# A hybrid decoder step on one core: the renewal of the recurrent states begins four weight slabs later and is spread over more slabs

## The chip, the core and the metric

The kernel runs on one core of a Trainium2 chip. The core has a matrix engine (TensorE, PE in the profile, with its weight loads listed apart as PEld), three engines for elementwise work (VectorE, DVE; ScalarE, ACT; GpSimd, POOL) and SyncE (SP), which here only issues DMA transfers. Each engine works through its own list of instructions in order, and they wait for each other by semaphores. Tiles lie in the on-chip memory SBUF; matmul results go to PSUM. The metric is the device time of one execution in microseconds (us), as a median over runs.

## The reference

One decoder layer, for 256 prompt tokens and 8 sample sequences of 8 tokens each (320 tokens in all), with a model width of 2048. Cut to what matters:

```python
def decoder_layer(x, ssm_state, ssm_conv_state, ffn_conv_state, p):
    h = rms_norm(x, p["norm_mix_pre"])
    proj = h @ p["w_in"]
    a_u, a_v, z, xbc, dt_raw = ...                      # columns of proj
    gate_out, chunk_v = chunk_spatial_gate(a_u, a_v, ...)
    ssm_out, new_ssm, new_ssm_conv = ssd_mixer(z, xbc, dt_raw, ssm_state, ...)
    mix = jnp.concatenate([gate_out, ssm_out], axis=-1) @ p["w_out"]
    x = x + rms_norm(mix, p["norm_mix_post"])
    f, new_ffn_conv = conv_ffn(rms_norm(x, p["norm_ffn_pre"]), ffn_conv_state, ...)
    return x + rms_norm(f, p["norm_ffn_post"]), new_ssm, ...

def conv_ffn(h, conv_state, w_up, conv_w, conv_b, w_down):
    up = h @ w_up                                       # 2048 -> 2 * 5632
    up, new_conv = causal_depthwise_conv(up, conv_state, conv_w, conv_b)   # 3 taps
    g, u = jnp.split(up, 2, axis=-1)
    return (jax.nn.gelu(g, approximate=True) * u) @ w_down, new_conv
```

Inside `ssd_mixer` each sample sequence has a recurrent state of 32 heads x 64 x 128 numbers. By the recurrence `h_t = exp(dt_t a) h_{t-1} + dt_t x_t B_t^T` over its eight tokens, the new state is the old one times a factor per head and sequence, plus a product of the token rows x and B. This new state is only an output; nothing in the layer reads it. The change concerns the work that makes it, called the renewal below.

## The kernel before, in words

**Weights in slabs.** Nearly all of the time goes into four large products. Their weights are float32, and each block of 128x128 is multiplied in three matmuls: `whi` by the high part of the activations (L143), `whi` by their low part (L144) and `wlo` by their high part (L145). The weights come in slabs of 512 KB. `slab()` issues one load on SP (L126, tile `wraw`), has ScalarE cast it to `whi` (L130) and VectorE subtract that from `wraw` to give `wlo` (L132). There are three buffers of each of these tiles, so at most three slabs are under way. One slab feeds 24 matmuls of 320 columns.

**The ConvFFN stage.** It runs from about 800 us to the end and has eleven groups of 512 columns. `ffn_up(g)` makes a group's up-projection in two halves, eight slabs each. After a half four accumulators in PSUM (`ps`) are evacuated, each by `evac`: POOL prepares the edges of the tile `pad` (L1084, L1085), VectorE multiplies the accumulator into it (L1087, L1088), ScalarE makes the first tap of the convolution (L1094) and VectorE two more (L1096, into `gcv` or `ucv`), POOL copies the last columns out (L1098, L1099), and gelu, product and split into `fhi` and `flo` follow. There are four PSUM banks for this, so the next half's accumulators wait until VectorE has read the old ones. `chunk_out(g)` is the down-projection of a group, eight slabs, whose results VectorE adds to `acc_ffn` (L236). The order is up(0), up(1), out(0), up(2), out(1) and so on: 24 slabs to a round.

**Work in the background.** A generator in the list `bg` is advanced by one step (`tick`) behind every slab; so each `yield` in it means "go on behind the next slab". In this way small work is placed between the slabs of large work. Slab loads, casts and subtractions are emitted at high priority and so stand a few slabs ahead of their matmuls in each engine's list.

**The renewals.** `renewals()` is such a generator. It is put into `bg` behind `ffn_up(0)`. It first finishes three prompt states (L1163, six yields), then issues on SP the load of `tote`, the factors of all heads (L1183), of the first four states (L1171, tile `st`, 256 KB each) and of the token rows (L1180, tile `xb`). Then, for each of four groups: it waits three slabs, ScalarE copies the token rows into `xb_parts` (L1191), VectorE completes these in two operations (L1194); and for each of two halves, POOL multiplies four states by their factors (L1199, one slab apart), the next states' loads are issued on SP, two slabs pass, TensorE makes the four products `up_ps` (L1211), VectorE adds each to its state (L1213) and ScalarE's queue stores it (L1215). States have four buffers for the first halves and two sets of three, shared with older tiles, for the second ones, so a load waits until the store of an older state has landed. All multiplications need `tote`.

A call of `finish(grow)` ahead of the last group would work off what is left of the generator at once; it comes behind 240 ticks. Before the change the generator ends at the 103rd.

Of the kernel before, what the change touches and what calls it, by code (L numbers as in the profile page):

```python
# [34 lines left out]
def hybrid_step(  # L35
# [21 lines left out]
    def misc(name):  # L57
        return ms.tile([P, 512], F32, tag="ms", name=name)
# [328 lines left out]
    def by_head(ap):  # L387
        return ap.rearrange("p (h d) -> p h d", d=64)
# [674 lines left out]
    with tc.tile_pool(name="fp", bufs=1) as fp:  # L1063
# [91 lines left out]
        def renewals():  # L1155

            raw = hp.tile([P, 4, NT], F32R, tag="ohi", name="xb").bitcast(F32).rearrange("p k n -> p (k n)").rearrange("p (h c) -> p h c", h=2)
            part = hp.tile([P, 4, NT], F32R, tag="olo", name="xb_parts").rearrange("p k n -> p (k n)").rearrange("p (h c) -> p h c", h=2)
            tote = fp.tile([P, NH, NB], F32, name="tote")
            for g, s1, x1d, _ in rest:  # L1160
                yield from repeat(None, 2)
                with tc.issue_after(rsqrt_ins[-1]):
                    dve.tensor_tensor(out=s1, in0=s1, in1=x1d, op=ALU.add)  # L1163
                act.dma_start(o_ssm_p[g], s1)

            def load(g, h):

                st = [fp.tile([P, 512], F32, tag="st", name="st", bufs=4) if h == 0 else
                      cp.tile([P, 512], F32, tag=("s1", "x1d")[i % 2], name="st", bufs=3) for i in range(4)]
                for i in range(4):  # L1170
                    sp.dma_start(st[i], state_ssm[4 * h + i, g])  # L1171
                return st

            def tokens(g):

                rows = xb_d[g].rearrange("(h i t) c -> i t h c", h=2, i=4)
                for i in range(4):
                    for r in range(4):
                        at = 32 * i + TS * r
                        sp.dma_start(raw[at:at + TS], rows[i])  # L1180

            with tc.issue_after(slab_load[-1]):
                sp.dma_start(tote, tote_d)  # L1183
                ahead = [load(0, 0)]
            yield
            with tc.issue_after(slab_load[-1]):
                tokens(0)
            for g in range(4):
                h0 = 8 * g
                yield from repeat(None, 3)  # L1190
                act.copy(part, raw)  # L1191
                yield
                for at, m in ((slice(0, 512), 0), (slice(512, 640), 1)):
                    dve.scalar_tensor_tensor(out=part[:, :, at], in0=part[:, :, at].bitcast(F32), scalar=low[:, m:m + 1], in1=raw[:, :, at],  # L1194
                                             op0=ALU.mult, op1=ALU.add)
                for h in range(2):
                    st = ahead.pop(0)
                    for i in range(4):
                        pool.tensor_tensor(out=by_head(st[i]), in0=by_head(st[i]),  # L1199
                                           in1=tote[:, h0:h0 + 8, 4 * h + i:4 * h + i + 1].to_broadcast([P, 8, 64]), op=ALU.mult)  # L1200
                        yield
                    if h == 0:
                        ahead.append(load(g, 1))
                    elif g < 3:
                        ahead.append(load(g + 1, 0))
                        tokens(g + 1)
                    yield from repeat(None, 2)
                    grown = [misc("up_ps") for _ in range(4)]
                    for i in range(4):
                        at = slice(32 * i, 32 * i + 32)  # L1210
                        pe.matmul(grown[i], part[at, h, 512:], part[at, h, :512], start=True, stop=True, tile_position=(32 * i, 0))  # L1211
                    for i in range(4):
                        dve.tensor_tensor(out=st[i], in0=st[i], in1=grown[i], op=ALU.add)  # L1213
                        yield
                        act.dma_start(o_ssm_s[4 * h + i, g], st[i])  # L1215

        NG = NF // 4
        nxt = ffn_up(0)
        grow = renewals()
        bg.append(grow)  # L1220
        for g in range(NG):
# [173 lines left out]
```

## Time and profile before

| | us |
|---|---|
| median of 3 runs | 1760.93 |
| lowest and highest run | 1760.37 and 1761.53 |
| the profiled execution, its own time | 1762.04 |
| its span, first to last instruction | 1760.3 |
| granted TensorE clock, mean | 0.999 |

The profile lists busy time by engine over the span. In a row of the timeline stand the start and the length in us, the engine, the line in the code, the operation, what it writes and reads, the shape, and how many instructions of the kind run without another in between; in brackets the idle time of the engine ahead of it and what ended that. DVE's share over the whole run is 66%, ACT's 46% and POOL's 15%. The 32 multiplications of L1199 take 41.0 us in all, the 32 additions of L1213 20.6 us, the eight operations of L1194 7.7 us and the 32 products of L1211 4.0 us.

### The profile page before, as it was taken

To read this page: it belongs to the slowest core of one execution; us is meant where nothing else is said; L and a number is where in the kernel's file an instruction comes from. 1 tells how busy PE (TensorE), PEld (TensorE's weight loads), DVE (VectorE), ACT (ScalarE), POOL (GpSimd) and SP (SyncE) were. 2 spreads that over 40 slices of the span, in tenths; PEclk is the share of its full clock that TensorE was granted. 3 is DMA by queue.
4 is the path that set the end of the run, shared out by engine and by line. 5 is a ranking of instruction groups with operands and counts; after the bars stand their busy time and mean duration, and the time that the engine had idled before them with its cause. 6 is when DMAs were issued, how large, how long until landed. Compare 5 with 4: busy or idle time off the path is not lost.

```text
span 1760.3 us, 31124 instructions
## 1 busy us (share of the span) xinstructions
PE 1751.6 (100%) x12178; PEld 1729.8 (98%) x12178; DVE 1154.1 (66%) x1949; ACT 806.6 (46%) x1172; POOL 272.7 (15%) x588
## 2 busy tenths in 40 slices
PE   9999999999999999999999999999999999999998
PEld 9999999999999999999999999999999999999997
DVE  7449754656767576668966677676657565656575
ACT  7344545333854445545544434343434343333335
POOL 1003200000111101021331212130201010111004
PEclk9999999999999999999999999999999999999999
DMA  7466655456665644554756666756454545454542
GB/s 248 144 167 182 185 151 150 153 155 190 216 206 163 201 145 131 166 161 143 228 169 223 189 217 195 222 185 192 151 153 148 156 148 155 148 155 147 155 151 104
DMA packets 228179, 301.38 MB, mean 171 GB/s; under 512 B 19936, under 2 KB 150848, under 8 KB 227840
## 3 DMA queue, kind: packets, MB, share of 16 engines
q1 hardware_dynamic: 215856, 281.27, 52.4%
q10 hardware_dynamic: 10640, 13.60, 2.2%
q0 software_dynamic: 1536, 4.52, 1.0%
q8 instruction: 96, 1.57, 0.4%
q14 instruction: 51, 0.42, 0.1%
HBM read 283.47 MB, written 15.61 MB: 170 GB/s over the span
## 4 chain that ended last, share of the span: by engine, by line
PE 95%; DVE 2%; DMA 1%; ACT 0%; POOL 0%; issue 0%; SPq 0%; POOLq 0%; DVEq 0%; ACTq 0%
PE ps L143 20%; PE ps L145 20%; PE ps L144 20%; PE pd L143 10%; PE pd L144 10%; PE pd L145 10%; PE y_ps L900 1%; DMA wraw<-in_ffn_w_up 1%; DVE wlo L132 1%; PE yo_ps L848 0%; PE sg L705 0%; PE tsum L284 0%; DVE h_lo L374 0%; DVE acc_mix L1042 0%; DMA vt<-in_xT 0%; ACT whi L130 0%
## 5 line engine op out<-in xcount | busy, mean ns | idle before, releaser
L132 DVE TENSOR_TENSOR wlo<-wraw,whi 128x1024 fp32r<-128x1024 f32 x470 | 582.9, 1241 | 436.9 <-ACT whi L130 434.9
L130 ACT CAST whi<-wraw 128x1024 fp32r<-128x1024 f32 x470 | 492.0, 1047 | 730.3 <-PE ps L144 437.7
L143 PE MATMUL ps<-h_hi,whi 128*128 128x320 f32 x2528 | 782.1, 310 | 0.4 <-ACT whi L130 0.4
L144 PE MATMUL ps<-h_lo,whi 128*128 128x320 f32 x2528 | 779.8, 309 | 0.0
L145 PE MATMUL ps<-h_hi,wlo 128*128 128x320 f32 x2528 | 777.8, 309 | 0.0
L143 PEld LDWEIGHTS ps<-h_hi,whi 128*128 128x128 f32 x2528 | 474.8, 188 | 4.2 <-issue 2.3
L144 PEld LDWEIGHTS ps<-h_lo,whi 128*128 128x128 f32 x2528 | 475.1, 188 | 0.0
L145 PEld LDWEIGHTS ps<-h_hi,wlo 128*128 128x128 f32 x2528 | 474.4, 188 | 0.1
L143 PE MATMUL pd<-fhi,whi 128*128 128x320 f32 x704 | 217.2, 309 | 0.0
L144 PE MATMUL pd<-flo,whi 128*128 128x320 f32 x704 | 217.0, 308 | 0.0
L145 PE MATMUL pd<-fhi,wlo 128*128 128x320 f32 x704 | 216.9, 308 | 0.0
L143 PE MATMUL pd<-ohi,whi 128*128 128x320 f32 x448 | 139.5, 312 | 0.0
L145 PE MATMUL pd<-ohi,wlo 128*128 128x320 f32 x448 | 138.5, 309 | 0.0
L144 PE MATMUL pd<-olo,whi 128*128 128x320 f32 x448 | 138.5, 309 | 0.0
L143 PEld LDWEIGHTS pd<-fhi,whi 128*128 128x128 f32 x704 | 132.2, 188 | 0.7 <-issue 0.7
L144 PEld LDWEIGHTS pd<-flo,whi 128*128 128x128 f32 x704 | 132.2, 188 | 0.2 <-issue 0.2
L145 PEld LDWEIGHTS pd<-fhi,wlo 128*128 128x128 f32 x704 | 132.2, 188 | 0.0
L1099 POOL COPY ptf<-pad 128x2 f32<-128x2 f32 x88 | 24.2, 275 | 508.3 <-DVE pad L1087 507.5
L236 DVE TENSOR_TENSOR acc_ffn<-acc_ffn,pd 128x320 f32<-128x320 f32 x160 | 77.2, 482 | 34.5 <-PE pd L145 33.6
L143 PEld LDWEIGHTS pd<-ohi,whi 128*128 128x128 f32 x448 | 84.0, 188 | 1.4 <-issue 0.7
L144 PEld LDWEIGHTS pd<-olo,whi 128*128 128x128 f32 x448 | 84.1, 188 | 0.2 <-issue 0.2
L145 PEld LDWEIGHTS pd<-ohi,wlo 128*128 128x128 f32 x448 | 84.1, 188 | 0.0
(301 smaller groups left out, 1513.6 us busy)
## 6 DMA issues: line engine op xcount, KB each, us to landing
wraw<-in_ffn_w_up SPq DMA_DIRECT2D x176, 512.0 KB
wraw<-in_w_in SPq DMA_DIRECT2D x142, 512.0 KB
wraw<-in_ffn_w_down SPq DMA_DIRECT2D x88, 512.0 KB
wraw<-in_w_out SPq DMA_DIRECT2D x64, 512.0 KB
st<-in_state_ssm SPq DMA_DIRECT2D x64, 256.0 KB
out_ssm_state_sample<-st ACTq DMA_DIRECT2D x32, 256.0 KB
cs<-dacs_d SPq DMA_DIRECT2D x16, 320.0 KB
xr<-in_xT SPq DMA_DIRECT2D x4, 640.0 KB
```

The lines of the kernel that those rows point to most:

```text
L130: act.copy(hi[:, :m], raw[:, :m])
L132: dve.tensor_tensor(out=lo[:, :m], in0=raw[:, :m], in1=hi[:, :m].bitcast(F32), op=ALU.subtract)
L143: pe.matmul(ps, whi, xhi, start=first, stop=False)
L144: pe.matmul(ps, whi, xlo, start=False, stop=False)
L145: newest[0] = pe.matmul(ps, wlo, xhi, start=False, stop=last).ins
L236: dve.tensor_tensor(out=acc[:, nb, :], in0=acc[:, nb, :], in1=ps[:, :NT], op=ALU.add)
L900: pe.matmul(ps[64 * i:64 * i + 64, cols], w(hl), x(hl, m, cpx), tile_position=(0, 64 * i), **flags)
L1099: pool.tensor_copy(ptf[:, k, :], pad[:, 256:258])
```

## The change

Three edits in `renewals()`, all of them yields:

```diff
@@ renewals()
                 act.dma_start(o_ssm_p[g], s1)
+            yield from repeat(None, 4)
...
             for g in range(4):
                 h0 = 8 * g
-                yield from repeat(None, 3)
+                yield from repeat(None, 3 if g else 12)
                 act.copy(part, raw)
                 yield
...
                         pool.tensor_tensor(out=by_head(st[i]), in0=by_head(st[i]),
                                            in1=tote[:, h0:h0 + 8, 4 * h + i:4 * h + i + 1].to_broadcast([P, 8, 64]), op=ALU.mult)
                         yield
+                        yield
```

The loads of `tote`, the states and the token rows are placed four slabs later; the first copy of the token rows is placed twelve slabs behind them instead of three; and two slabs, not one, pass at each multiplication. The generator now ends at the 148th tick. No operation is added or taken away. A line is added ahead of the loads, so line numbers behind it rise by one in the changed kernel, and by two behind the third edit (the loads are L1184, L1172 and L1181, the multiplications L1200, the products L1213 there).

Each engine's list is the same in kind and number; the places change. On SP, this is where `tote`, the first states and the first token rows are issued, beside the weight loads `wraw`. Before:

```order
L126 DMA wraw<-in_ffn_w_up 128x2x512 x2
L126 DMA wraw<-in_ffn_w_up 128x4x256
L1183 DMA tote<-tote_d 128x256
L1171 DMA st<-in_state_ssm 128x512 x3
L126 DMA wraw<-in_ffn_w_up 128x4x256
L1171 DMA st<-in_state_ssm 128x512
L1180 DMA xb<-xb_d 8x2x640
```

After:

```order
L126 DMA wraw<-in_ffn_w_up 128x2x512 x2
L126 DMA wraw<-in_ffn_w_up 128x4x256
L1172 DMA st<-in_state_ssm 128x512
L126 DMA wraw<-in_ffn_w_up 128x4x256
L1172 DMA st<-in_state_ssm 128x512
L126 DMA wraw<-in_ffn_w_up 128x2x512 x3
L1184 DMA tote<-tote_d 128x256
L1172 DMA st<-in_state_ssm 128x512 x2
L126 DMA wraw<-in_ffn_w_up 128x2x512
L1172 DMA st<-in_state_ssm 128x512 x2
L1181 DMA xb<-xb_d 8x2x640
```

`tote` stands four weight loads later. Two states are now loaded ahead of it.

On POOL, these are the first multiplications, among the preparation of `pad` and the copies from it. Before:

```order
L1084 MEMSET pad 128x2
L1085 COPY pad<-fst 128x8x2
L1199 TENSOR_TENSOR st<-st,tote 128x512 x5
L1084 MEMSET pad 128x2
L1085 COPY pad<-fst 128x8x2
L1199 TENSOR_TENSOR st<-st,tote 128x512 x3
L1099 COPY ptf<-pad 128x2
L1098 COPY stg<-pad 128x16
```

After:

```order
L1084 MEMSET pad 128x2
L1085 COPY pad<-fst 128x8x2
L1200 TENSOR_TENSOR st<-st,tote 128x512
L1098 COPY stg<-pad 128x16
L1099 COPY ptf<-pad 128x2
L1200 TENSOR_TENSOR st<-st,tote 128x512 x4
L1098 COPY stg<-pad 128x16
L1099 COPY ptf<-pad 128x2
L1200 TENSOR_TENSOR st<-st,tote 128x512 x3
L1099 COPY ptf<-pad 128x2
L1098 COPY stg<-pad 128x16
L1200 TENSOR_TENSOR st<-st,tote 128x512
```

Eight multiplications stood together, ahead of the copies of a half's tiles; now ten (the last one stands behind one more preparation of `pad`) stand among the copies of the next half's tiles.

On VectorE, these are the two operations on `xb_parts`, among the subtractions that make `wlo`, behind the end of group 1's evacuation. Before:

```order
L371 TENSOR_TENSOR flo<-a,fhi 128x320
L132 TENSOR_TENSOR wlo<-wraw,whi 128x1024 x2
L1194 TENSOR_SCALAR xb_parts<-xb_parts,low,xb 128x2x512
L1194 TENSOR_SCALAR xb_parts<-xb_parts,low,xb 128x2x128
L132 TENSOR_TENSOR wlo<-wraw,whi 128x1024
L1213 TENSOR_TENSOR st<-st,up_ps 128x512 x4
```

After:

```order
L371 TENSOR_TENSOR flo<-a,fhi 128x320
L132 TENSOR_TENSOR wlo<-wraw,whi 128x1024 x6
L1195 TENSOR_SCALAR xb_parts<-xb_parts,low,xb 128x2x512
L1195 TENSOR_SCALAR xb_parts<-xb_parts,low,xb 128x2x128
L132 TENSOR_TENSOR wlo<-wraw,whi 128x1024 x6
```

They stand four slabs later, and the additions that need the first products no longer follow one slab behind them. On TensorE the first four products stood in the sixth slab of `chunk_out(0)`; they now stand three slabs into the second half of `ffn_up(2)`, fourteen slabs later. Without them TensorE's list is the same row for row.

## The prediction

> **What bounds the kernel now.** I read the page first, then the busy time by stretches, then TensorE's waits.
>
> ```profile
> PE 1751.6 (100%) x12178; PEld 1729.8 (98%) x12178; DVE 1154.1 (66%) x1949; ACT 806.6 (46%) x1172; POOL 272.7 (15%) x588
> ...
> 920.00:950.00 30.00, 29.41 (x202) 28.94 (x201) 23.72 (x38) 17.61 (x30) 6.32 (x15) 1.00 0.61 193
> ...
> 1150.00:1250.00 100.00, 100.00 (x683) 99.12 (x682) 66.08 (x108) 40.68 (x51) 15.44 (x49) 1.00 0.56 173
> 1250.00:1350.00 100.00, 100.00 (x684) 100.00 (x683) 59.42 (x98) 39.04 (x47) 12.86 (x40) 1.00 0.49 150
> ```
>
> Behind each stretch stand its length and the busy time of PE, PEld, DVE, ACT and POOL. TensorE is busy throughout at full clock. 684 matmuls in 100 us are one every 0.146 us; a slab (one 512 KB weight load) feeds 24 of them, so TensorE eats a slab in 3.51 us. The renewals run from 853 to 1229 us. The stretch with them (1150 to 1250) has 683 matmuls, the one after them 684, and in both TensorE is never idle. So whatever the change does, time can come only from an idle gap of TensorE that goes, or go into a new one. Its waits, whole run, longest first (total, times, longest):
>
> ```profile
> PE early L70 <- DVE ones L66: 1.1, 1, 1.1
> PE tsum L284 <- DVE sq L302: 0.7, 1, 0.7
> PE up_ps L1211 <- DVE xb_parts L1194: 0.6, 1, 0.6
> PE ps L143 <- ACT whi L130: 0.4, 1, 0.4
> ```
>
> Only one of them belongs to the renewals: 0.6 us, once. That is the most the change can win, 0.03% of the run.
>
> **Part 1: the wait that goes.** Here is that gap, in the timeline:
>
> ```profile
> 938.08 2.48 DVE L1194 SCALAR_TENSOR_TENSOR xb_parts<-xb_parts,low,xb 128x1024 fp32r<-128x1024 f32 x2 [0.26 <-DMA wraw<-in_ffn_w_up]
> 938.89 2.60 POOL L1199 TENSOR_TENSOR st<-st,tote 128x512 f32<-128x512 f32 x2 [8.41 <-DMA st<-in_state_ssm]
> ...
> 940.71 0.50 PE L1211 MATMUL up_ps<-xb_parts 32*128 32x512 f32 x4 [0.59 <-DVE xb_parts L1194]
> ```
>
> VectorE's two operations on xb_parts end at 940.56, and the first group of up_ps matmuls, already next on TensorE, waits 0.59 us for them. In the changed order these two operations stand behind four more slabs on VectorE, but the first up_ps group stands some fourteen slabs later on TensorE, so about ten slabs (35 us) more lie between them. The wait goes whole: minus 0.6. What is late next there is nothing: TensorE's weights are ready.
>
> **Part 2: what only moves.** The 32 up_ps matmuls, the xb casts on ScalarE, the 32 additions on VectorE and the 32 stores are the same in number; without up_ps, TensorE's order is the same row for row. I cost these at nothing. Their cover is the lead with which weights are made ready. It can be read from an undisturbed piece after the last renewal:
>
> ```profile
> 1229.15 0.37 SPq L126 DMA_DIRECT2D wraw<-in_ffn_w_up  x1
> ...
> 1237.20 1.03 ACT L130 CAST whi<-wraw 128x1024 fp32r<-128x1024 f32 x1
> ...
> 1247.46 1.05 ACT L130 CAST whi<-wraw 128x1024 fp32r<-128x1024 f32 x1 [2.47 <-PE ps L144]
> ...
> 1248.54 1.23 DVE L132 TENSOR_TENSOR wlo<-wraw,whi 128x1024 fp32r<-128x1024 f32 x1 [2.29 <-ACT whi L130]
> ```
>
> A cast starts when TensorE lets go of the slab three back (1247.46); two slabs, 7.0 us, then lie ahead of the new one, and its wlo is read two matmuls (0.3) in, at 1254.7. It is made at 1249.77: 4.9 us early. If VectorE or ScalarE lose less than 4.9 us together, TensorE sees nothing; each us beyond costs one.
>
> The state loads on SP wait until the store that frees their buffer has landed, and weight loads queue behind them. SP's waits in 850 to 1300 us say how long:
>
> ```profile
> SPq L1171 <- DMA out_ssm_state_sample<-st: 14.8, 8, 4.4
> ```
>
> At most 4.4 us at once, and TensorE felt none of it. A weight load is issued 8.05 us ahead of its cast (1229.15 to 1237.20, the same slab) and needs about 4.8 us to land (the figure of tote below, my estimate for a slab), so 3.2 us of lateness are free and 4.9 more before TensorE stops. In the new order the loads again stand two or three slabs behind their stores. Cost nothing; if a block grew beyond 8 us, it would cost the rest. The end of the chain moves from the 103rd slab behind ffn_up(0) to the 148th; the call that would finish it by force comes after the 240th, so nothing is left over for it.
>
> **Part 3: what the first multiplications meet.** This is the term that decides. All of POOL's multiplications wait for tote, then run in a bunch. Before:
>
> ```profile
> 870.97 0.37 SPq L126 DMA_DIRECT2D wraw<-in_ffn_w_up  x1
> 871.39 0.50 SPq L1183 DMA_DIRECT2D tote<-tote_d  x1
> ```
> ```profile
> 876.22 6.63 POOL L1199 TENSOR_TENSOR st<-st,tote 128x512 f32<-128x512 f32 x5 [0.77 <-DMA tote<-tote_d]
> ...
> 883.21 5.06 POOL L1199 TENSOR_TENSOR st<-st,tote 128x512 f32<-128x512 f32 x3
> ```
> ```profile
> 876.32 1.37 DVE L1096 SCALAR_TENSOR_TENSOR ucv<-pad,prm,ucv 128x336 f32<-128x336 f32 x1
> 877.62 2.08 DVE L132 TENSOR_TENSOR wlo<-wraw,whi 128x1024 fp32r<-128x1024 f32 x1
> ...
> 883.38 5.97 DVE L132 TENSOR_TENSOR wlo<-wraw,whi 128x1024 fp32r<-128x1024 f32 x3 [0.19 <-ACT whi L130]
> ```
>
> Tote lands 4.83 us after its issue, and eight multiplications follow. VectorE beside them is slow: 1.37 us for L1096 and 2.08, then 1.99 each, for wlo. Alone they take 0.57 and 1.22 (rows below), so each VectorE operation that meets a multiplication loses 0.8 (0.77 to 0.86). There it met the end of the previous half's evacuation and cost TensorE nothing.
>
> The change puts tote's load four weight loads later, 14 us, and lets ten multiplications stand in this bunch instead of eight, since two states of the next group were loaded early. The next half's evacuation comes at that moment. Its undisturbed shape, 96 slabs later, is on VectorE:
>
> ```profile
> 1232.09 0.42 DVE L1087 TENSOR_TENSOR pad<-ps,r 128x256 f32<-128x256 f32 x1
> ...
> 1233.44 0.57 DVE L1096 SCALAR_TENSOR_TENSOR gcv<-pad,prm,gcv 128x336 f32<-128x336 f32 x1 [0.80 <-ACT gcv L1094]
> ...
> 1234.46 1.22 DVE L132 TENSOR_TENSOR wlo<-wraw,whi 128x1024 fp32r<-128x1024 f32 x1
> ...
> 1236.07 1.04 DVE L1096 SCALAR_TENSOR_TENSOR gcv<-pad,prm,gcv 128x336 f32<-128x336 f32 x2
> ...
> 1237.50 1.03 DVE L1096 SCALAR_TENSOR_TENSOR gcv<-pad,prm,gcv 128x336 f32<-128x336 f32 x2
> 1238.46 1.22 DVE L132 TENSOR_TENSOR wlo<-wraw,whi 128x1024 fp32r<-128x1024 f32 x1
> 1239.59 1.64 DVE L1096 SCALAR_TENSOR_TENSOR gcv<-pad,prm,gcv 128x336 f32<-128x336 f32 x3
> 1241.50 1.22 DVE L132 TENSOR_TENSOR wlo<-wraw,whi 128x1024 fp32r<-128x1024 f32 x1 [0.27 <-ACT whi L130]
> ```
>
> On this clock tote follows the weight load of 1229.15, so it is issued at 1229.57 and lands at 1234.40. From there to the wlo of 1241.50 VectorE has ten operations on SBUF tiles (three wlo, seven L1096). Eight multiplications stand ready ahead of it; the last two stand behind the copies of the third accumulator and behind later loads. Eight times 0.8 is 6.4 us; 0.3 us of free time (the gap ahead of 1241.50) takes some of it; 6.1 remain against the lead of 4.9. TensorE waits 1.2 us. VectorE also empties the fourth accumulator late, on which the next half waits; that stall would be part of the same 1.2, for while TensorE stands VectorE catches up.
>
> Bounds: nothing lost at all, if the multiplications come scattered. A case for this is a later bunch of before, four multiplications into the same evacuation, of which TensorE felt nothing:
>
> ```profile
> 1146.10 4.11 POOL L1199 TENSOR_TENSOR st<-st,tote 128x512 f32<-128x512 f32 x3 [0.20 <-DMA st<-in_state_ssm]
> ```
> ```profile
> 1146.90 0.41 DVE L1087 TENSOR_TENSOR pad<-ps,r 128x256 f32<-128x256 f32 x1
> ...
> 1148.25 1.04 DVE L1096 SCALAR_TENSOR_TENSOR gcv<-pad,prm,gcv 128x336 f32<-128x336 f32 x1 [0.80 <-ACT gcv L1094]
> ```
>
> L1096 lost 0.47 there, and L1087, which reads PSUM, nothing. From above: each operation loses a whole multiplication, 1.06 us (the sum of 883.21, less what POOL itself waited; 5.06 for three is at least that). I take 0.8, for the bunch at 876 is the nearest in length.
>
> [...]
>
> The later bunches of the new order fall, by the places of their loads, ahead of an evacuation or beside its first operations, as those of before did: nothing.
>
> **The sum.** Profiled execution: 1762.04 us, of which the span is 1760.3. Minus 0.6, plus 1.2, is 1762.6. The median of the runs is 1760.93, 1.1 below the profiled one, so 1761.5.
>
> **Rivals.**
> 1. Forecast: the gap goes, the bunch costs 1.2: 1761.5. Chance 0.48.
> 2. The bunch is scattered, as states land one by one, and the lead holds: 1760.3. For it: four multiplications into an evacuation cost nothing. Against: ten, of which six have states loaded long before. 0.32.
> 3. Each of eight blocks by its full 1.06: 8.5 - 0.3 - 4.9 = 3.3 lost, 1763.6. For it: 1.99 per wlo is not far off. 0.08.
> 4. Slower by over 0.2%: all ten multiplications count at their full length ahead of that wlo: 10.6 - 0.3 - 4.9 = 5.4 lost, 1765.7. It decides from 9.3 us of blocking on (4.9 + 0.3 + 0.6 + 3.5). Against: POOL itself waits between them for VectorE's pads. 0.07.
> 5. A state load blocks SP. To cost 3.5 beyond the 0.6 won, it must hold a weight load for 12.2 us, nearly three times the longest wait of 4.4: about 1764.5. 0.03.
> 6. Faster by over 0.2%: no gap of that size is there to win; 0.02 for what I do not see.
>
> **How the numbers follow.** 0.2% is 3.5 us, about what a measurement of this kernel can tell from no change; cases 1 to 3 lie inside. So same 0.88, slower 0.10, faster 0.02. The range takes in cases 1 to 3 with the scatter of the runs (1760.37 to 1761.53): 1759.9 to 1763.8.
>
> **What would show it.** Right: the row "up_ps <- xb_parts" is gone from TensorE's waits; L1200 (the multiplications) begins near 890 us instead of 876, with VectorE's wlo and L1096 at about twice their time until 903; TensorE waits there, for wlo or for pad, by about a microsecond in all. Part 3 is wrong if no such wait stands near 893 to 905; part 2 is wrong if TensorE waits anywhere behind 910; the whole is wrong if the span moves by more than 3.5 us.

## The result, and the profile after

The changed kernel takes 1766.06 us (median of 8 runs, 1764.73 to 1767.02), the one before 1760.93 (1760.37 to 1761.53): 5.1 us slower, ratio 1.0027 with a 95% interval from 1.0018 to 1.0037. The forecast was 1761.5, its range ended at 1763.8, and "slower by over 0.2%" had a chance of 0.10. The profiled execution took 1765.90 us, with a span of 1764.2.

I read the profile after in the order in which I had read the one before. TensorE's waits over the whole run come first (total, times, longest):

```profile
PE ps L143 <- ACT whi L130: 2.5, 2, 2.2
PE early L70 <- DVE ones L66: 1.1, 1, 1.1
PE ps L145 <- DVE wlo L132: 0.7, 1, 0.7
...
PE ps L143 <- DVE pad L1088: 0.2, 1, 0.2
```

The row "up_ps <- xb_parts" is gone, as forecast. A wait of 2.2 us for `whi` is new: ScalarE's tile, not VectorE's. The busy time by stretches says where (columns as before). The kernel before:

```profile
888.00:915.00 27.00, 27.00 (x186) 27.00 (x185) 15.53 (x24) 11.99 (x16) 5.40 (x17) 1.00 0.60 181
```

The changed kernel:

```profile
888.00:915.00 27.00, 23.84 (x149) 23.07 (x148) 17.33 (x20) 10.24 (x14) 16.20 (x26) 0.94 0.51 155
```
```profile
906.70:910.60 3.90, 3.90 (x16) 3.90 (x17) 2.36 (x2) 1.29 (x2) 0.00 (x0) 0.56 0.67 181
...
950.00:1250.00 300.00, 300.00 (x2045) 297.80 (x2045) 194.87 (x306) 121.69 (x147) 61.60 (x132) 1.00 0.62 192
```

All of the loss lies between 888 and 915: 149 matmuls instead of 186. 37 matmuls of 0.146 us are 5.4 us; less the 0.6 won at the old gap, that makes 4.8 of the 5.1. (The two spans differ by 3.9 only: the profiled execution of the kernel before was 1.1 above its median, with a wait of 0.7 for `sq` at 849, ahead of the first edit, that the changed kernel's does not show.) Behind 950 nothing is lost: 2045 matmuls in 300 us, as before. Inside the stretch there are two losses: TensorE stands still, and then runs at a granted clock of 0.56 for four microseconds. In its timeline:

```profile
902.87 0.31 PE L145 MATMUL ps<-h_hi,wlo 128*128 128x320 f32 x1
905.40 0.41 PE L143 MATMUL ps<-h_hi,whi 128*128 128x320 f32 x1 [2.23 <-ACT whi L130]
905.65 0.31 PE L144 MATMUL ps<-h_lo,whi 128*128 128x320 f32 x1
906.66 0.42 PE L145 MATMUL ps<-h_hi,wlo 128*128 128x320 f32 x1 [0.70 <-DVE wlo L132]
...
907.34 0.47 PE L145 MATMUL ps<-h_hi,wlo 128*128 128x320 f32 x1
907.61 0.47 PE L143 MATMUL ps<-h_hi,whi 128*128 128x320 f32 x1
...
910.51 0.31 PE L145 MATMUL ps<-h_hi,wlo 128*128 128x320 f32 x1
```

By the starts, 2.4 us are lost ahead of 905.40 and 0.9 ahead of 906.66. Then a matmul starts every 0.27 us instead of 0.146 until 910.51: some 1.7 us more. The rest of the 5.4 is mostly a wait for `pad` ahead of 895.02 (0.4).

Why was `whi` late? ScalarE's timeline of the changed kernel:

```profile
895.73 0.49 ACT L1101 ACTIVATE gcv<-gcv 128x336 f32<-128x336 f32 x1
903.85 0.34 ACTq L1143 DMA_DIRECT2D out_ffn_conv_sample<-stg  x1
904.30 1.04 ACT L130 CAST whi<-wraw 128x1024 fp32r<-128x1024 f32 x1 [8.09 <-POOL pad L1084]
```

ScalarE idles for 8.09 us. What stands next on its queue is no calculation but the issue of a store, L1143, which sends the half's `stg` to memory. It waits for GpSimd's copies into `stg` (L1098), and the cast of the next weights stands behind it. GpSimd at that time:

```profile
888.13 1.06 POOL L1200 TENSOR_TENSOR st<-st,tote 128x512 f32<-128x512 f32 x1 [11.17 <-DMA tote<-tote_d]
...
889.70 5.63 POOL L1200 TENSOR_TENSOR st<-st,tote 128x512 f32<-128x512 f32 x4
...
896.18 4.62 POOL L1200 TENSOR_TENSOR st<-st,tote 128x512 f32<-128x512 f32 x3
...
901.31 1.06 POOL L1200 TENSOR_TENSOR st<-st,tote 128x512 f32<-128x512 f32 x1
...
902.50 1.06 POOL L1200 TENSOR_TENSOR st<-st,tote 128x512 f32<-128x512 f32 x1
903.50 0.18 POOL L1099 COPY ptf<-pad 128x2 f32<-128x2 f32 x1
903.62 0.20 POOL L1098 COPY stg<-pad 128x16 f32<-128x16 f32 x1
```

The fourth copy of `stg` stands behind all ten multiplications and ends at 903.82; the store is issued at 903.85. (The bracket of the cast names `pad` L1084, which stands right behind that copy on GpSimd; the store reads `stg`, and in the runs with five slabs and with eight ahead below, the bracket there names the copy of `stg` itself.) Before, the same store on ScalarE's queue:

```profile
895.25 0.34 ACTq L1143 DMA_DIRECT2D out_ffn_conv_sample<-stg  x1
895.81 0.47 ACT L1101 ACTIVATE gcv<-gcv 128x336 f32<-128x336 f32 x1
896.79 1.05 ACT L130 CAST whi<-wraw 128x1024 fp32r<-128x1024 f32 x1 [0.51 <-ACT gcv L1101]
```

There the multiplications ended at 888.3, ahead of the half's copies, and nothing was held.

### The profile page after: what moved, and what is told of

It is laid out like the page before. It is cut to its first block, busy times and chain, and to the rows that moved or that the text cites. A ratio compares the mean times of both kernels' runs of the same rounds, so it can differ in the third digit from the quotient of the medians.

```text
span 1764.2 us, 31108 instructions
## 1 busy us (share of the span) xinstructions
PE 1753.4 (99%) x12178; PEld 1730.8 (98%) x12178; DVE 1151.4 (65%) x1949; ACT 808.3 (46%) x1172; POOL 270.3 (15%) x588
## 4 chain that ended last, share of the span: by engine, by line
PE 97%; POOL 1%; DVE 1%; ACT 0%; issue 0%; DMA 0%; SPq 0%; POOLq 0%; ACTq 0%; DVEq 0%
PE ps L143 21%; PE ps L145 21%; PE ps L144 21%; PE pd L143 10%; PE pd L145 10%; PE pd L144 10%; PE y_ps L900 1%; PE yo_ps L848 0%; PE sg L705 0%; PE tsum L284 0%; DVE wlo L132 0%; PE vt_ps L590 0%; POOL st L1200 0%; POOL acc_ffn L1273 0%; PE xt_ps L385 0%; ACT whi L130 0%
```

## The experiments

Theory A, from these rows: multiplications on GpSimd, copies of `stg` behind them, a store on ScalarE that waits for the copies, a cast behind the store, TensorE. Theory B is the forecast's: the multiplications slow VectorE. Theory C: the wider spacing costs in itself. All ratios are to the kernel before, run beside them on the same chip (1761.21 us for the first four, 1761.12 for the others).

**The store out of the way.** The changed kernel, with that one store behind the next half's first L1094 on ScalarE (`first_u`; diffs are cut, and lines in profiles of the experiments are numbered as in the code of each):

```diff
...
-                act.dma_start(o_fconv_s[:, k:k + 4], stg[:, half])
+                with tc.issue_after(first_u[0]) if g == 1 and half == 0 else nullcontext():
+                    act.dma_start(o_fconv_s[:, k:k + 4], stg[:, half])
```

> The changed kernel, with one store moved: the first half's out_ffn_conv_sample<-stg of ffn_up(1) stands on ScalarE's queue behind the next half's first L1094 (about 28 us later), not ahead of a cast. Theory A (ScalarE is held: this store waits for GpSimd's copies L1098, which stand behind ten multiplications, and the next cast of weights stands behind the store): the wait for whi goes, the granted clock stays at 1.00, nothing is lost between 890 and 912, and the time is 1760.3, 0.6 below before, or 1760.9 if the wait for xb_parts won nothing. Theory B (the multiplications slow VectorE, as forecast): VectorE's order is untouched, so most of the loss stays: 1763 to 1766.

Measured: 1761.38 us, ratio 1.0001 (0.9992 to 1.0010), 0.5 above the higher value of theory A. ScalarE's timeline, the first and the last of GpSimd's ten multiplications, and TensorE's waits from 885 to 1400 us:

```profile
896.82 0.49 ACT L1104 ACTIVATE gcv<-gcv 128x336 f32<-128x336 f32 x1
897.21 1.04 ACT L130 CAST whi<-wraw 128x1024 fp32r<-128x1024 f32 x1
```
```profile
889.23 1.06 POOL L1204 TENSOR_TENSOR st<-st,tote 128x512 f32<-128x512 f32 x1 [11.28 <-DMA tote<-tote_d]
...
905.57 2.05 POOL L1204 TENSOR_TENSOR st<-st,tote 128x512 f32<-128x512 f32 x1
```
```profile
PE ps L143 <- DVE pad L1089: 0.3, 1, 0.3
```

The cast follows the gelu (L1104) at once, though GpSimd's ten multiplications still run from 889 to 907. The wait for `whi` is gone, and so are the fall of the clock and the loss against before. A is shown and B refuted for all but a small rest: 0.3 us of waiting for `pad`, which VectorE empties late; by the starts TensorE loses 0.6 us there. The time is 1.0 us above the fastest kernels below (1760.34 to 1760.43), but that is less than the intervals can tell apart, and one of those kernels (no first edit) has a wait of 0.2 for `pad` too. So how much of the 1.0 is VectorE's is not shown.

**Which edit.** Without the first edit, the other two kept:

```diff
-            yield from repeat(None, 4)
```

> The changed kernel without its first edit (no four slabs ahead of the loads); the twelve slabs and the second yield stay. Eight multiplications then stand ahead of the first copies of the half, as before. Theory A: the store of stg comes as early as before, no wait for whi; the wait of 0.6 for xb_parts goes: 1760.3. Theory C (the wider spacing of the later renewals, with their loads and stores, costs something spread over the round trip): 1762 or more, with no single wait to be seen.

Measured: 1760.43 us, ratio 0.9996 (0.9987 to 1.0004). And the first edit alone, on the kernel before:

```diff
+            yield from repeat(None, 4)
```

> The kernel before, with the first edit alone (four slabs ahead of the loads). Eight multiplications, not ten, then stand ahead of the last copy of stg. Theory A: the store is issued two multiplications (2.5 us) earlier than in the changed kernel, at about 901.4, so the cast ends at about 902.9, just in time; wlo is late by 0.7 us or less, the clock stays at 1.00: 1761.0 to 1761.7. Theory B: VectorE is slowed in the same place as in the changed kernel, so nearly all of the loss is there: 1764 to 1766.

Measured: 1766.15 us, ratio 1.0025 (1.0015 to 1.0035): the whole loss. So the first edit makes it, and the other two cost nothing; theory C falls. The expectation missed, because its count was wrong: in this kernel's timeline of GpSimd ten multiplications stand ahead of the last copy too, in the same groups as in the changed kernel, so A should have said the same time. With the same hold ahead of the cast comes the same time:

```profile
888.83 1.06 POOL L1200 TENSOR_TENSOR st<-st,tote 128x512 f32<-128x512 f32 x1 [11.46 <-DMA tote<-tote_d]
...
890.39 5.63 POOL L1200 TENSOR_TENSOR st<-st,tote 128x512 f32<-128x512 f32 x4
...
896.87 4.62 POOL L1200 TENSOR_TENSOR st<-st,tote 128x512 f32<-128x512 f32 x3
```
```profile
904.53 0.34 ACTq L1143 DMA_DIRECT2D out_ffn_conv_sample<-stg  x1
904.99 1.04 ACT L130 CAST whi<-wraw 128x1024 fp32r<-128x1024 f32 x1 [8.08 <-POOL pad L1084]
```

**One slab more.**

```diff
-            yield from repeat(None, 4)
+            yield from repeat(None, 5)
```

> The changed kernel with five slabs ahead of the loads instead of four. tote lands 3.5 us later, and ten multiplications still stand ahead of the last copies of stg. Theory A: the store and the cast behind it come 3.5 us later, so TensorE waits about 5.9 us for whi instead of 2.4, and the slow clock behind it costs about 2 again: 1769 to 1770.5. Theory B: fewer of VectorE's operations of this evacuation meet a multiplication, so the loss is smaller than 5: 1762 to 1765.

Measured: 1761.27 us, ratio 1.0001 (0.9992 to 1.0010). Both expectations missed, A by 8 us. Its premise did not hold: GpSimd's list was rearranged with the loads, and its timeline has only five multiplications ahead of the last copy of `stg`:

```profile
892.00 1.06 POOL L1200 TENSOR_TENSOR st<-st,tote 128x512 f32<-128x512 f32 x1 [0.80 <-issue]
...
893.57 1.06 POOL L1200 TENSOR_TENSOR st<-st,tote 128x512 f32<-128x512 f32 x1
...
895.00 3.39 POOL L1200 TENSOR_TENSOR st<-st,tote 128x512 f32<-128x512 f32 x2
...
898.76 1.40 POOL L1200 TENSOR_TENSOR st<-st,tote 128x512 f32<-128x512 f32 x1
900.11 0.47 POOL L1098 COPY stg<-pad 128x16 f32<-128x16 f32 x1
```

The store is then issued at 900.61 instead of 903.85. That fits the chain of A, read afterwards: TensorE has no wait for `whi` here, and one of 0.6 us for `wlo`. But the length of the queue came by accident in this run, so I set it by hand.

**Eight and twelve instead of ten.** Eight: two multiplications held behind the fourth copy.

```diff
+                        with tc.issue_after(fourth[0]) if (g, h) == (1, 1) else nullcontext():
                             pool.tensor_tensor(out=by_head(st[i]), in0=by_head(st[i]), ...)
```

> The changed kernel, with two of the ten multiplications (the first two states of group 1's second half) held on GpSimd's queue behind the fourth copy of stg: eight stand ahead of it, all else as in the changed kernel. Theory A: the store of stg is issued about 2.7 us earlier, at 901.2, the cast ends at about 902.7, in time; wlo is late by about 0.6 us; too short for the clock to fall. 1760.7 to 1761.5. If the lateness of TensorE does not come from the length of this queue: 1765 to 1766.5, as the changed kernel.

Twelve: three more multiplications of the same size, into a tile that is not read; two of them stand ahead of the fourth copy.

```diff
+                        if g == 0 and h == 0:
+                            for _ in range((0, 1, 1, 1)[i]):
+                                pool.tensor_tensor(out=by_head(spare), in0=by_head(st[i]), ...)
```

> The changed kernel with three more multiplications of the same size into a spare tile that nobody reads; two of them stand ahead of the fourth copy of stg, so twelve in place of ten. Theory A: the store and the cast come 2.2 to 2.7 us later than in the changed kernel; TensorE waits about 4.8 us for whi. If the slow clock behind a wait has a fixed length (about 5 us, a loss of about 2.1): 1768.3 to 1768.9. If its loss grows with the wait (twice the wait, twice the loss): 1770 to 1771.

Measured: eight 1763.26 us, ratio 1.0013 (1.0004 to 1.0022); twelve 1769.14, ratio 1.0046 (1.0032 to 1.0059). Both expectations missed: eight lies 1.8 us above its range, twelve between the two ranges that it told apart. With eight, ScalarE's store, VectorE's late `wlo`, and TensorE's waits over the whole run:

```profile
902.59 0.34 ACTq L1147 DMA_DIRECT2D out_ffn_conv_sample<-stg  x1
```
```profile
904.13 4.05 DVE L132 TENSOR_TENSOR wlo<-wraw,whi 128x1024 fp32r<-128x1024 f32 x3 [2.90 <-ACT whi L130]
```
```profile
PE ps L145 <- DVE wlo L132: 1.2, 2, 1.0
...
PE ps L143 <- ACT whi L130: 0.7, 2, 0.4
```

Of these, 1.0 us for `wlo` and 0.2 for `whi` fall here, between 903 and 906. With twelve, and the stretch from 908 to 912 us of it:

```profile
905.99 0.34 ACTq L1143 DMA_DIRECT2D out_ffn_conv_sample<-stg  x1
```
```profile
PE ps L143 <- ACT whi L130: 4.1, 1, 4.1
```
```profile
908.00:912.00 4.00, 3.64 (x14) 3.24 (x14) 3.11 (x3) 2.15 (x3) 0.00 (x0) 0.50 0.54 147
```

The first multiplication begins at 888.84 with eight, 888.13 with ten and 888.39 with twelve, so the store is issued 13.8, 15.7 and 17.6 us behind it, and the time is 1763.3, 1766.1 and 1769.1. A's direction holds at each step. Its size for eight was off by 2 us: taking two away brought the store forward by 2.0 us, counted from the first multiplication, not 2.7, and the three late `wlo` took 4.05 us instead of 3.59, beside the two that were held and the copies behind them. With twelve, TensorE waits nearly twice as long as with ten. Of its 56 missing matmuls (130 of 186 between 888 and 915, 8.2 us) the starts put 2.3 us to the slow pace behind the last wait, against 1.7 with ten: the loss grows, but by less than the wait.

**Later still.** Eight slabs instead of four, so that the ten multiplications fall behind the half's copies:

```diff
-            yield from repeat(None, 4)
+            yield from repeat(None, 8)
```

> The changed kernel with eight slabs ahead of the loads instead of four: the ten multiplications fall behind the evacuation of the first half, all the copies of stg of that half stand ahead of them. Theory A: no store waits behind them, nothing is lost: 1760.3 to 1760.9. If it is the later start as such that costs (the renewals pushed into a busier stretch): 1766 or more.

Measured: 1760.38 us, ratio 0.9995 (0.9986 to 1.0004). In its timeline the ten run without a pause, and the store is long out:

```profile
902.80 14.26 POOL L1200 TENSOR_TENSOR st<-st,tote 128x512 f32<-128x512 f32 x10 [5.35 <-DMA tote<-tote_d]
```
```profile
893.97 0.34 ACTq L1143 DMA_DIRECT2D out_ffn_conv_sample<-stg  x1
```

So neither the later start nor the bunch costs anything that can be measured; its place among the copies does.

**The second edit alone**, on the kernel before:

```diff
-                yield from repeat(None, 3)
+                yield from repeat(None, 3 if g else 12)
```

> The kernel before with the second edit alone (twelve slabs ahead of the first copy of the token rows). Theory A: the multiplications stay where they were before, and the wait of 0.6 us for xb_parts goes: 1760.3 to 1760.6, a candidate to beat both kernels, by less than a run scatters. Theory C (a longer round trip of the renewals costs in itself): 1762.

Measured: 1760.34 us, ratio 0.9997 (0.9988 to 1.0006). Three kernels without the wait for `xb_parts` and without the hold (this one, no first edit, eight slabs) lie 0.74 to 0.78 us below before. Each interval takes in 1, so none is shown to beat before by itself; all three are 5.6 to 5.7 us below the changed kernel.

## Why the prediction was wrong

- **Part 1 was right.** The wait for `xb_parts` is gone. The three kernels above lie 0.7 to 0.8 us below before, which fits the 0.6 that was forecast, though none of them is shown to be faster.
- **Part 2 was right on SP.** Its waits for landed stores in the changed kernel, 860 to 1450 us, are no longer at once than before (4.4 at most), and TensorE felt none of them (2045 matmuls between 950 and 1250 in both kernels):

```profile
SPq L1172 <- DMA out_ssm_state_sample<-st: 21.2, 12, 4.4
```

- **Part 3 had the place and the cause, and the wrong way from there to TensorE.** The multiplications began at 888.13 (forecast: near 890), ten in a bunch, and TensorE waited between 893 and 907. VectorE was slowed as forecast: three L1096 in 3.93 us instead of 1.64.

```profile
894.80 1.38 DVE L1096 SCALAR_TENSOR_TENSOR gcv<-pad,prm,gcv 128x336 f32<-128x336 f32 x2
896.10 1.21 DVE L132 TENSOR_TENSOR wlo<-wraw,whi 128x1024 fp32r<-128x1024 f32 x1
897.23 3.93 DVE L1096 SCALAR_TENSOR_TENSOR gcv<-pad,prm,gcv 128x336 f32<-128x336 f32 x3
```

- **The step that failed is the sum of part 3, where only VectorE's lateness counts against the lead of 4.9 us.** Part 2 had said that VectorE and ScalarE count together; ScalarE was then put at nothing without a look at what its queue waits for. What was left out is who else waits for GpSimd. The copies L1098 stood in the quoted order right behind the multiplications; a store on ScalarE needs them, and ScalarE's casts stand behind the store. Held for 8.1 us, ScalarE passed on to TensorE a wait of 2.2 us for `whi` and one of 0.7 for `wlo`, 3.3 us by the starts. By the forecast's own rule, each microsecond beyond the lead, 8.1 less 4.9 is 3.2: the lead was right, the term was missing. With the store moved, 5.1 us over before became 0.2.
- The term that stood in the sum, VectorE's, did not act as forecast. VectorE's eight L1096 and two `wlo` of this bunch lost 4.8 us (estimated against the same operations in the run with eight slabs, where no multiplication runs beside them), not 6.1, and that is inside the lead. VectorE was through before the cast and stood idle until it came:

```profile
905.38 1.23 DVE L132 TENSOR_TENSOR wlo<-wraw,whi 128x1024 fp32r<-128x1024 f32 x1 [4.22 <-ACT whi L130]
```

- With the store moved no `wlo` is late, and the wait for `pad` is all that is seen of VectorE. That the forecast's 1761.5 is close to the 1761.38 of that run is luck.
- A second term was missing: behind these waits of 2.2 and 0.7 us TensorE did not go on at full pace; the granted clock was 0.56 in the 3.9 us that followed. About 1.7 us of the loss are the slow clock.
- **Rival 4's 1765.7 is near the measured time by accident.** It had VectorE lose 10.6 us; VectorE's operations in the bunch lost about half of that, and hardly any of it reached TensorE. Rivals 2, 3 and 5 did not happen.

## What to carry to other kernels

When work is moved on an engine, list not only its own operations but each instruction behind it that another engine waits for, and then what stands behind that waiting instruction. The issue of the store took 0.34 us here and lies inside the 8.09 us that the profile gives as ScalarE's idle time, yet it held the casts behind it on its queue for as long as its source was late. A bunch moved by zero or eight slabs cost nothing here and by four slabs 5 us: look for what it lands among.

## What the runs showed of the hardware

The granted clock fell to about half behind TensorE's waits of 2.2 and 0.7 us with two matmuls between them (changed kernel: 0.56 in the quoted 3.9 us, 1.00 from 910.6 us on), and behind one of 4.1 with one of 0.4 after it (twelve ahead: 0.72 from 906 to 908 us, 0.50 from 908 to 912, 0.57 from 912 to 914, 1.00 from 914 to 916). Counted from the last wait, the price of the slow pace was 1.7 and 2.3 us by the starts. The clock stayed at 1.00 behind waits of 0.2 and 1.0 us with two matmuls between them (eight ahead, 902 to 916 us), behind one of 0.6 (five slabs, 902 to 912), and behind the 0.59 ahead of 940.71 in the kernel before (912 to 950). How long a wait must be for the clock to fall, and what brings it back, these runs do not show.

GpSimd was slower beside VectorE too: one of its multiplications took 1.06 us with VectorE idle (901.31; VectorE stood from 901.16 to 905.38) and 1.4 to 1.5 on average beside VectorE's operations (5.63 for four, 4.62 for three). At 1.06 each, by this estimate, the ten would take 10.6 us instead of 13.4; whether TensorE would then have waited at all was not tried.
